# One layer with two token mixers on one core: the second half's output projection as seven block products, with weight sums, a scaled x and another chunk order

## The chip, the core and the metric

The kernel runs on one core of one Trainium2 chip. The metric is the device time of one execution in microseconds, the median of a few runs. TensorE (PE) multiplies, VectorE (DVE) and ScalarE (ACT) do elementwise work and empty PSUM, GpSimd (POOL) does elementwise work on SBUF, and SyncE (SP) issues nearly all DMAs, in order, each after the semaphores that it waits for.

## What is computed

The reference, cut to its skeleton (2048 tokens, width 2048, float32):

```
h = rms_norm(x, norm_w)
q, k, v, z_attn, u, z_ssm = split(h @ w_in)
o_attn = sliding_window_attention(q, k, v) * silu(z_attn)        # 16 heads, 4 kv heads, blocks of 128
y = gelu(ssm(u));  y = y * sigmoid(y @ w_glu + b_glu)            # 64 groups, complex diagonal state
o_ssm = y * silu(z_ssm)
merged = concat(rms_norm(o_attn, g_a), rms_norm(o_ssm, g_s))     # 1024 + 1024 columns
out = x + merged @ w_out                                         # w_out 2048 x 2048
```

## The kernel before

Tokens are worked on in two halves of 1024. Every float32 operand of a large product is cut into a high part (a cast to the fast matmul type, on ACT) and a low part (the rest, a subtraction on DVE); a product is three matmuls: high by high, high by low, low by high. Weights arrive as pieces of 256 KB in a tile `wr` (three buffers) in `w_unit` (lines 310 to 319), and become `wh` and `wl`. With `panel_feat` a piece feeds 24 matmuls of 512 columns, with `panel_tok` 48 of 256 columns.

`run` (lines 1013 to 1070) lays down panels and side work, which `weave` spreads over them with a raised priority; a list scheduler then fixes the order on each engine. In order of time:

- First half: the input projection, beside `setup_all` (line 1078): the rotary tables, the statistics of the second half's x (`x_stats`) and `ssm_setup` (line 580), whose last part (lines 743 to 768) builds the tables `TCS` in DRAM.
- Attention of the first half beside the panels of z. Between the two halves `x_later` (line 297) makes the second half's x: a row of 1/rms spread over the partitions by eight small matmuls (`spread`), then for each of 16 tiles a load of `xT`, a scaling on DVE, a cast on ACT and a subtraction on DVE.
- The second half's projections beside `ssm_pairs`, which leaves y in the order of chunks: a column is (t, c), and token 8c + t.
- For each half: `glu` (line 903) with `tail_attn` (line 872) as side work, both emptying into tiles that `split` cuts in two. In `glu` the tile `tt` has one buffer and is written twice for each half panel; y stays in chunk order until `split`, which reorders.
- The first half's output projection (`out_panel`), beside the second half's attention; the second half's (`out_wide`, line 957), which has PE to itself: 4 column blocks x 2 halves of K x 8 k x 8 row blocks x 3 = 1536 matmuls of 512 columns. The norms' row scales are applied to the finished sums, as they are read from PSUM, by one DVE instruction with x as the addend (line 977).

All loads and stores stand in one queue, SP's, in the scheduler's order.

## Time and profile before

| | |
|---|---|
| median of 3 runs | 2885.39 us (2884.41 to 2886.68) |
| profiled execution | 2888.56 us, span 2886.8 us |
| PE busy | 2801.0 us, 97% of the span |
| DVE, ACT, POOL busy | 1897.9, 961.3, 205.0 us |
| granted TensorE clock, mean | 0.992 |
| HBM traffic | 271.03 MB read, 99.55 MB written |

A view by windows gives the busy time of each engine in a stretch, with the number of instructions, the granted clock as a share of 2.4 GHz, the share of the DMA engines' time and their rate. In a timeline each line is a start, a duration, the engine, the line of the program and what is written and read; in square brackets stands the idle time before it and what ended it. SPq is SP's queue: its duration is that of issuing, not of the transfer.

### The profile page before, as it was taken

To read this page: it belongs to the slowest core of one execution; us is meant where nothing else is said; L and a number is where in the kernel's file an instruction comes from. 1 tells how busy PE (TensorE), PEld (TensorE's weight loads), DVE (VectorE), ACT (ScalarE), POOL (GpSimd) and SP (SyncE) were. 2 spreads that over 40 slices of the span, in tenths; PEclk is the share of its full clock that TensorE was granted. 3 is DMA by queue.
4 is the path that set the end of the run, shared out by engine and by line. 5 is a ranking of instruction groups with operands and counts; after the bars stand their busy time and mean duration, and the time that the engine had idled before them with its cause. 6 is when DMAs were issued, how large, how long until landed. Compare 5 with 4: busy or idle time off the path is not lost.

```text
span 2886.8 us, 45269 instructions
## 1 busy us (share of the span) xinstructions
PE 2801.0 (97%) x16992; PEld 2502.2 (87%) x16992; DVE 1897.9 (66%) x4419; ACT 961.3 (33%) x2089; POOL 205.0 (7%) x341
## 2 busy tenths in 40 slices
PE   6989999989999899999999999998999999999999
PEld 5879999878888688888999988878999999778887
DVE  6682746856773976677679985378999884842222
ACT  6421212134442543333323332345444433521110
POOL 0000000001110112000000000000222220000000
PEclk9999999999999999999999999999999999999999
DMA  5842536553332532544355555343444436333321
GB/s 175 237 117 69 158 92 168 142 142 112 94 115 75 183 115 84 159 144 146 120 156 148 154 156 145 101 138 96 136 143 124 124 106 186 107 104 106 106 78 57
DMA packets 421290, 369.34 MB, mean 128 GB/s; under 512 B 53200, under 2 KB 377296, under 8 KB 421072
## 3 DMA queue, kind: packets, MB, share of 16 engines
q1 hardware_dynamic: 419008, 366.45, 42.9%
q8 instruction: 134, 2.20, 0.3%
q14 instruction: 84, 0.69, 0.1%
q10 hardware_dynamic: 2064, 0.01, 0.0%
HBM read 271.03 MB, written 99.55 MB: 128 GB/s over the span
## 4 chain that ended last, share of the span: by engine, by line
PE 81%; DVE 9%; DMA 6%; issue 2%; ACT 1%; SPq 1%; ACTq 0%; DVEq 0%; POOL 0%; POOLq 0%
PE psg L331 31%; PE psg L349 30%; PE psg L966 6%; PE pss L966 3%; DMA oa<-OA 2%; PE pso L562 2%; PE pss L522 2%; PE pst L966 2%; PE pso L966 1%; DVE ml L93 1%; DVE yg L84 1%; PE pst L547 1%; PE pss L797 1%; DVE wl L84 1%; DVE accs L84 1%
## 5 line engine op out<-in xcount | busy, mean ns | idle before, releaser
L84 DVE TENSOR_TENSOR wl<-wr,wh 128x512 fp32r<-128x512 f32 x456 | 314.6, 690 | 539.6 <-ACT wh L317 530.4
L317 ACT CAST wh<-wr 128x512 fp32r<-128x512 f32 x456 | 282.6, 620 | 1028.3 <-PE psg L331 331.6
L331 PE MATMUL psg<-xl,wh 128*128 128x512 f32 x1536 | 495.3, 395 | 5.2 <-DVE xl L84 5.2
L331 PE MATMUL psg<-xh,wl 128*128 128x512 f32 x1536 | 493.1, 394 | 4.8 <-DVE wl L84 4.7
L331 PE MATMUL psg<-xh,wh 128*128 128x512 f32 x1536 | 492.1, 395 | 3.0 <-ACT wh L317 2.4
L349 PE MATMUL psg<-wh,xh 128*128 128x256 f32 x1536 | 434.2, 284 | 1.8 <-ACT rx L395 1.8
L349 PE MATMUL psg<-wl,xh 128*128 128x256 f32 x1536 | 435.1, 284 | 0.3 <-DVE wl L84 0.3
L349 PE MATMUL psg<-wh,xl 128*128 128x256 f32 x1536 | 433.5, 284 | 0.0
L331 PEld LDWEIGHTS psg<-xl,wh 128*128 128x128 f32 x1536 | 287.9, 189 | 63.7 <-DVE xl L84 7.2
L331 PEld LDWEIGHTS psg<-xh,wl 128*128 128x128 f32 x1536 | 287.5, 189 | 63.0 <-DVE wl L84 6.6
L331 PEld LDWEIGHTS psg<-xh,wh 128*128 128x128 f32 x1536 | 288.0, 190 | 60.8 <-ACT wh L317 3.3
L349 PE MATMUL psg<-wh,mh 128*128 128x256 f32 x1024 | 289.5, 286 | 8.6 <-ACT tt L914 7.7
L349 PEld LDWEIGHTS psg<-wh,xh 128*128 128x128 f32 x1536 | 293.8, 192 | 2.1 <-ACT rx L395 2.0
L349 PEld LDWEIGHTS psg<-wl,xh 128*128 128x128 f32 x1536 | 294.3, 192 | 0.7 <-DVE wl L84 0.7
L349 PEld LDWEIGHTS psg<-wh,xl 128*128 128x128 f32 x1536 | 293.5, 192 | 0.0
L349 PE MATMUL psg<-wl,mh 128*128 128x256 f32 x1024 | 289.7, 284 | 0.7 <-DVE wl L84 0.7
L349 PE MATMUL psg<-wh,ml 128*128 128x256 f32 x1024 | 288.4, 285 | 0.0
L84 POOL TENSOR_TENSOR pm<-ph,sel 128x256 fp32r<-128x256 f32 x240 | 193.1, 825 | 957.6 <-ACT ph L550 612.9
L349 PEld LDWEIGHTS psg<-wh,mh 128*128 128x128 f32 x1024 | 194.7, 191 | 9.4 <-ACT tt L914 7.9
L349 PEld LDWEIGHTS psg<-wl,mh 128*128 128x128 f32 x1024 | 195.9, 191 | 0.9 <-DVE wl L84 0.9
L349 PEld LDWEIGHTS psg<-wh,ml 128*128 128x128 f32 x1024 | 194.7, 191 | 0.0
L539 ACT ACTIVATE sm<-pss,mx,rs 128x128 f32<-128x128 f32 x240 | 108.3, 458 | 93.6 <-DVE mx L93 87.7
(396 smaller groups left out, 4606.6 us busy)
## 6 DMA issues: line engine op xcount, KB each, us to landing
wr<-in_w_in_dram SPq DMA_DIRECT2D x296, 256.0 KB
wr<-in_w_out_dram SPq DMA_DIRECT2D x128, 256.0 KB
tb<-TCS SPq DMA_DIRECT2D x64, 256.0 KB
xr<-in_x_dram SPq DMA_DIRECT2D x64, 256.0 KB
out_dram<-xr SPq DMA_DIRECT2D x64, 256.0 KB
raw<-MBC SPq DMA_DIRECT2D x32, 384.0 KB
kst<-KK SPq DMA_DIRECT2D x56, 192.0 KB
xst<-in_x_dram SPq DMA_DIRECT2D x16, 512.0 KB
```

The costliest lines, as they stand in the source:

```text
L84: (eng or self.nc.vector).tensor_tensor(out=out, in0=a, in1=b, op=op)
L93: self.nc.vector.scalar_tensor_tensor(out=out, in0=a, scalar=s, in1=b, op0=op0, op1=op1)
L317: nc.scalar.copy(hi, raw)
L331: nc.tensor.matmul(ps[t], wt[:, kk, :], xx[k][:, t * 512:(t + 1) * 512], start=(k == 0 and i == 0), stop=(k == nkc - 1 and i == 2))
L349: nc.tensor.matmul(o, xx[k][:, sl], wt[:, kk, :], start=(k == 0 and i == 0 and t % 2 == 0), stop=(k == nkc - 1 and i == 2), skip_group_che ...
L522: nc.tensor.matmul(ps[:, h * 256:h * 256 + 256], qst[:, bq % 2, hp * 2 + h, :], kst[:, i, ksl], start=(h == 0 and i == 0), stop=(i == 1), ...
L539: nc.scalar.activation(sm[:, h, :], sc[:, h, :], AF.Exp, scale=rs[:, h:h + 1], bias=negm[:, h:h + 1], accum_out=den[:, h:h + 1])
L547: nc.tensor.transpose(pt[:, h * P:(h + 1) * P], sm[:, h, :], self.ident)
L562: nc.tensor.matmul(po, vst[:, blk + kb, :], pm[:, i, kb], start=(i == 0 and kb == 0), stop=(i == 1 and kb == 1))
L797: nc.tensor.matmul(o, m[:, g, 0:128], u[:, g, 384:640], start=(g == 0 and i == 0), stop=(i == 2), skip_group_check=True)
L966: nc.tensor.matmul(ps[t], xx[k0 + k][:, t * P:(t + 1) * P], wt[:, 0, :], start=(k == 0 and j == 0), stop=(k == 7 and j == 2))
```

## The change

The second half's output projection is cut into 2 x 2 blocks of tokens, K and columns (each 512 x 1024 x 1024) and computed by the scheme of Strassen and Winograd: seven products in place of eight, with sums of weight blocks and of activation blocks as operands. `product` works one off in two column blocks of 512: 16 weight pieces of 256 KB, 12 matmuls of 512 columns for each; 7 x 16 x 12 = 1344 matmuls in all.

- The four sums of weight blocks (`out_sums`) are made beside `ssm_setup`, three steps for each of its steps, in 32 units (8 K-tiles x 4 pieces of 256 columns): 6 loads, 4 subtractions on POOL and 4 stores of 128 KB a unit, through two tiles `ws0` and `ws1` of one buffer each, into `WT` in DRAM.
- The scales of the norms can no longer be applied to finished sums. So `attn_scale` multiplies the attention output by its row scale on POOL during the first half's last panel and stores it (`OAN`); the sum of squares for it is gathered in `attend` (`asq`). The SSM part is scaled in `ssm_side`. The `form_...` generators make the left operands as side work of the products.
- Finished blocks are kept in `ac` tiles; `final` adds the last product to them on DVE, and x on POOL.
- `x_scaled` makes x times 1/rms for the second half beside the tables (POOL, to `XN` in DRAM); `x_later` then loads it and needs one ACT and one DVE instruction for a tile.
- `glu` writes its result into the tile of z, in token order, so that `split` no longer reorders; `tt` is written once for each half panel.
- `attend`: the mask on the probabilities is applied to one of the two key blocks, with the difference of the values (`dv`) as the other operand: two masked products in place of four, one on POOL and one on DVE; the division by the denominator moves from DVE to ACT. The second half's attention is spread over the first 0.7 of the panels, from 0.5.

```diff
-    def x_later(self, half, pool):
+    def x_scaled(self, pool, half):
         rb = pool.tile([P, HT], F32, tag="rb", name="rb")
         self.spread(self.rstd[:, half * 8:half * 8 + 8], rb, pool)
         for k in range(NK):
+            x = pool.tile([P, HT], F32, tag="xs", name="xs", bufs=2)
+            self.ld.dma_start(x, self.a["xT"][k * P:(k + 1) * P, half * HT:half * HT + HT])
+            self.tt(x, x, rb, ALU.mult, self.nc.gpsimd)
+            self.st.dma_start(self.XN[k], x)
+            yield
+
+    def x_later(self):
+        nc = self.nc
+        for k in range(NK):
             x = self.stage("xq")
-            self.ld.dma_start(x, self.a["xT"][k * P:(k + 1) * P, half * HT:half * HT + HT])
-            self.stt(x, x, self.nw[:, k:k + 1], rb, ALU.mult, ALU.mult)
-            nc.scalar.copy(self.xh[k], x)
-            self.tt(self.xl[k], x, self.xh[k].bitcast(F32), ALU.subtract)
+            self.ld.dma_start(x, self.XN[k])
+            w = self.nw[:, k:k + 1]
+            nc.scalar.activation(self.xh[k], x, AF.Copy, scale=w)
+            self.stt(self.xl[k], x, w, self.xh[k].bitcast(F32), ALU.mult, ALU.subtract)
...
+    def attn_scale(self, pool):
+        for k in range(8):
+            o = self.stage("on")
+            self.ld.dma_start(o, self.OA[k * P:(k + 1) * P, HT:SEQ])
+            self.tt(o, o, self.rba, ALU.mult, self.nc.gpsimd)
+            self.st.dma_start(self.OAN[k], o)
+            yield
...
+    def form_s2(self):
+        for k in range(8):
+            o = self.attn_scaled(k, 0, HT)
+            a1, a2 = o[:, 0:512], o[:, 512:HT]
+            w, wn = self.aow[:, k:k + 1], self.aown[:, k:k + 1]
+            self.stt(a2, a2, w, self.ssm_view(k, 1), ALU.mult, ALU.add)
+            self.stt(a1, a1, wn, a2, ALU.mult, ALU.add)
+            self.split_to(0, k, a1)
+            v = self.ssm_view(k, 0)
+            self.tt(v, v, a1, ALU.subtract)
+            yield
...
+    def out_sums(self, pool):
+        nc = self.nc
+        g = nc.gpsimd
+        for u in range(32):
+            k, c = u // 4, u % 4 * 256
+            x, y = (pool.tile([P, 256], F32, tag=f"ws{i}", name=f"ws{i}") for i in range(2))
+            get = lambda t, q: self.ld.dma_start(t, self.w_block(q, k, c, 256))
+            put = lambda i, t: self.st.dma_start(self.WT[i, k, :, c:c + 256], t)
+            get(x, 1)
+            get(y, 0)
+            self.tt(x, x, y, ALU.subtract, g)
+            put(0, x)
+            get(y, 3)
+            self.tt(y, y, x, ALU.subtract, g)
+            put(1, y)
+            yield
+            get(x, 2)
+            self.tt(x, y, x, ALU.subtract, g)
+            put(3, x)
+            get(x, 1)
+            get(y, 3)
+            self.tt(y, y, x, ALU.subtract, g)
+            put(2, y)
+            yield
...
+    def product(self, slot, q, evac, *sides):
+        for n in range(2):
+            ps = [self.psg() if n == 0 else self.psa() for t in range(4)]
+            for k in range(8):
+                raw = self.wp.tile([P, 512], F32, tag="wr", name="wr")
+                self.ld.dma_start(raw, self.w_block(q, k, n * 512, 512))
...
+                for t in range(4):
+                    sl = slice(o + t * P, o + t * P + P)
+                    for j, (xx, wt) in enumerate(((self.sh[c], hi), (self.sh[c], lo), (self.sl[c], hi))):
+                        nc.tensor.matmul(ps[t], xx[:, sl], wt, start=(k == 0 and j == 0), stop=(k == 7 and j == 2))
...
+            for t in range(4):
+                evac(n, t, ps[t])
...
+        B11, B12, B21, B22, T1, T2, T3, T4 = range(8)
+        ssm, s2, s1 = ssm_side(), self.form_s2(), self.form_s1()
+        s4, a22 = self.form_view(2, 0), self.form_view(0, 1)
+        self.product(0, B11, e1, (self.form_s3(), 8, 0), (ssm, 5, 6))
+        self.product(1, T3, e7, (ssm, 5, 0), (s2, 3, 10))
+        self.product(2, B21, e2, (s2, 5, 0))
+        self.product(0, T2, e6, (s1, 8, 0))
+        self.product(1, T1, e5, (s4, 8, 0))
+        self.product(2, B22, e3, (a22, 8, 0))
+        self.product(0, T4, e4)
...
                 zv = sz.rearrange("p (c t) -> p t c", t=8)[:, t * 4:t * 4 + 4, :]
-                ov = o.rearrange("p (t c) -> p t c", t=4)
-                self.tt(ov, ov, zv, ALU.mult)
-                f = lambda x: x.rearrange("p (c t) -> p t c", t=8)[:, t * 4:t * 4 + 4, :]
+                self.tt(zv, o.rearrange("p (t c) -> p t c", t=4), zv, ALU.mult)
+                if t == 0:
+                    return
                 if m == 0:
-                    nc.scalar.activation(f(acc), ov, AF.Square)
+                    nc.scalar.activation(acc, sz, AF.Square)
                 else:
-                    nc.scalar.activation(tt, o, AF.Square)
-                    self.tt(f(acc), f(acc), tt.rearrange("p (t c) -> p t c", t=4), ALU.add)
+                    sq = self.stage("sq")
+                    nc.scalar.activation(sq, sz, AF.Square)
+                    self.tt(acc, acc, sq, ALU.add)
...
+        with self.tc.tile_pool(name="bg", bufs=1) as pool:
+            sums = self.out_sums(pool)
+            for _ in self.ssm_setup():
+                for _ in range(3):
+                    next(sums, None)
+                yield
```

What the scheduler makes of it is shown at two places. The first is SP beside the SSM setup: `MBC<-Bm` and `MBC<-Cm` are stores of `ssm_setup`, `wr<-in_w_in_dram` are the weight pieces that PE lives on. Before:

```order
L314 DMA wr_3499<-in_w_in_dram 128x2x256 [waits DMAHW7_49,DVE_49]
L724 DMA MBC_85<-Bm_3282 128x4x128 [waits DMAHW0_49,Activation_49]
L731 DMA MBC_85<-Cm_3734 128x4x128 [waits DMAHW1_49,DVE_49]
L314 DMA wr_3553<-in_w_in_dram 128x2x256 [waits DMAHW2_49,DVE_49]
L724 DMA MBC_85<-Bm_3489 128x4x128 [waits DMAHW3_49,Activation_49]
L731 DMA MBC_85<-Cm_3985 128x4x128 [waits DMAHW4_49,DVE_49]
L468 DMA VS_84<-vs_3292 128x2x512 [waits DMAHW5_49,DVE_49]
L468 DMA VS_84<-vs_3296 128x2x512 [waits DMAHW6_49,DVE_49]
L724 DMA MBC_85<-Bm_3730 128x4x128 [waits DMAHW7_49,Activation_49]
```

and in the changed kernel, one unit of `out_sums` from its first load to its last store:

```order
L1005 DMA ws0_3776<-in_w_out_dram 128x256 [waits DMAHW5_49]
L1005 DMA ws1_3777<-in_w_out_dram 128x256 [waits DMAHW2_49,DMAHW0_49]
L1006 DMA WT_90<-ws0_3776 128x256 [waits DMAHW3_49,Pool_49]
L1005 DMA ws1_3777<-in_w_out_dram 128x256 [waits DMAHW4_49,DMAHW2_49]
L323 DMA wr_4872<-in_w_in_dram 128x2x256 [waits DVE_49]
L1006 DMA WT_90<-ws1_3777 128x256 [waits DMAHW6_49,Pool_49]
L1005 DMA ws0_3776<-in_w_out_dram 128x256 [waits DMAHW7_49,DMAHW3_49]
L323 DMA wr_4926<-in_w_in_dram 128x2x256 [waits DVE_49]
L1006 DMA WT_90<-ws0_3776 128x256 [waits DMAHW1_49,Pool_49]
L1005 DMA ws1_3777<-in_w_out_dram 128x256 [waits DMAHW6_49]
L1005 DMA ws0_3776<-in_w_out_dram 128x256 [waits DMAHW1_49]
L1006 DMA WT_90<-ws1_3777 128x256 [waits DMAHW4_49,Pool_49]
```

A store to `WT` waits for POOL (`Pool`), and so for the loads ahead of it; the load into `ws1` in the second row waits for the store ahead of the unit to have landed (`DMAHW0`), and the load into `ws0` in the last but one for the store two rows ahead of it (`DMAHW1`). Two weight pieces stand behind these waits in the same queue.

The second place is ACT at the end of the second half's `glu`, up to the first casts of the output projection's weights (`tt` lines 914 and 924 before; 1160 after). Before:

```order
L869 ACTIVATE mh14_27091<-yg6_25864,sow_613 128x4x128
L924 ACTIVATE tt_26929<-yg6_25864 128x512
L869 ACTIVATE mh14_27091<-yg6_25864,sow_613 128x4x128
L317 CAST wh_27202<-wr_27200 128x512
L914 ACTIVATE tt_27009<-psg_26947,bgh_617 128x512
L924 ACTIVATE tt_27009<-yg7_25870 128x512
L869 ACTIVATE mh15_27097<-yg7_25870,sow_613 128x4x128
L914 ACTIVATE tt_27015<-psg_26948,bgh_617 128x512
L924 ACTIVATE tt_27015<-yg7_25870 128x512
L869 ACTIVATE mh15_27097<-yg7_25870,sow_613 128x4x128
L317 CAST wh_27232<-wr_27230 128x512
L317 CAST wh_27262<-wr_27260 128x512
```

and now:

```order
L1160 ACTIVATE tt_27673<-psg_27611,bgh_619 128x512
L1160 ACTIVATE tt_27677<-psg_27612,bgh_619 128x512
L1171 ACTIVATE sq_27681<-sz_27609 128x1024
L1043 CAST wh_27793<-wr_27791 128x512
L929 ACTIVATE fh3_27686<-ob_27684,aow_613 128x512
L1043 CAST wh_27818<-wr_27816 128x512
L1160 ACTIVATE tt_27754<-psg_27692,bgh_619 128x512
L1160 ACTIVATE tt_27758<-psg_27693,bgh_619 128x512
L1171 ACTIVATE sq_27762<-sz_27690 128x1024
L929 ACTIVATE fh3_27686<-ob_27765,aow_613 128x512
L1043 CAST wh_27836<-wr_27834 128x512
L1043 CAST wh_27859<-wr_27857 128x512
```

The two tanh of a panel (`tt<-psg`, which free its two banks) now follow one another, with no `split` of y between them, and the weights of the first product are cast ahead of the last panel's tanh.

## Rows read from the trace of the kernel before

**Rows 1.** The profile's page: its first line and two lines of section 1.

```profile
span 2886.8 us, 45269 instructions
PE 2801.0 (97%) x16992; PEld 2502.2 (87%) x16992; DVE 1897.9 (66%) x4419; ACT 961.3 (33%) x2089; POOL 205.0 (7%) x341
```

**Rows 2.** Windows of 72 us: stretch, length, PE, PEld, DVE, ACT, POOL busy (instructions), clock, DMA.

```profile
936.00:1008.00 72.00, 60.67 (x278) 47.87 (x277) 64.21 (x121) 35.89 (x74) 11.61 (x10) 0.95 0.61 187
1008.00:1080.00 72.00, 72.00 (x359) 60.78 (x359) 51.33 (x158) 32.48 (x99) 11.83 (x16) 0.98 0.38 109
```

**Rows 3.** The same view, the ends of the two `glu` stages.

```profile
1872.00:1944.00 72.00, 68.63 (x300) 55.87 (x299) 50.39 (x60) 36.85 (x54) 0.00 (x0) 1.00 0.46 145
1944.00:2016.00 72.00, 62.14 (x437) 58.32 (x436) 58.63 (x111) 37.51 (x62) 0.20 (x1) 0.95 0.33 97
2448.00:2520.00 72.00, 68.07 (x303) 55.28 (x302) 57.24 (x66) 39.88 (x58) 0.00 (x0) 1.00 0.38 117
2520.00:2592.00 72.00, 65.31 (x278) 52.57 (x278) 38.62 (x67) 21.66 (x29) 0.00 (x0) 0.93 0.31 101
```

**Rows 4.** The same view with 20 us windows, short idle times at full clock.

```profile
580.00:600.00 20.00, 16.46 (x72) 12.98 (x70) 10.78 (x13) 1.25 (x2) 0.00 (x0) 1.00 0.60 159
```

**Rows 5.** Waits of PE: who waited for whom, us in total, times, longest.

```profile
PE psg L331 <- ACT tt L914: 8.6, 7, 1.7
PE psg L349 <- ACT tt L914: 7.7, 1, 7.7
```

**Rows 6.** Timeline of PE in `out_wide`, the first and last of 29 lines.

```profile
2699.63 0.39 PE L966 MATMUL psg<-wl,mh 128*128 128x512 f32 x1
...
2705.97 0.39 PE L966 MATMUL pss<-wh,ml 128*128 128x512 f32 x1
```

**Rows 7.** The page, section 5: subtraction and cast of a weight piece.

```profile
L84 DVE TENSOR_TENSOR wl<-wr,wh 128x512 fp32r<-128x512 f32 x456 | 314.6, 690 | 539.6 <-ACT wh L317 530.4
L317 ACT CAST wh<-wr 128x512 fp32r<-128x512 f32 x456 | 282.6, 620 | 1028.3 <-PE psg L331 331.6
```

**Rows 8.** Timelines of SP and DVE: two stores and the instructions that wait for them.

```profile
345.15 0.36 SPq L731 DMA_DIRECT2D MBC<-Cm  x1
348.32 0.69 DVE L84 TENSOR_TENSOR Cm<-C,PR 128x512 f32<-128x512 f32 x1 [1.14 <-DMA MBC<-Cm]
367.62 0.37 SPq L731 DMA_DIRECT2D MBC<-Cm  x1
369.92 0.69 DVE L84 TENSOR_TENSOR Cm<-C,PR 128x512 f32<-128x512 f32 x1 [1.01 <-DMA MBC<-Cm]
```

**Rows 9.** Timelines of SP and ACT: two loads and the instructions that wait for them.

```profile
597.17 0.39 SPq L314 DMA_DIRECT2D wr<-in_w_in_dram  x1
600.84 0.62 ACT L317 CAST wh<-wr 128x512 fp32r<-128x512 f32 x1 [9.64 <-DMA wr<-in_w_in_dram]
2452.34 0.32 SPq L879 DMA_DIRECT2D oa<-OA  x1
2456.29 1.34 ACT L869 ACTIVATE mh<-oa,aow 128x512 fp32r<-128x512 f32 x2 [0.88 <-DMA oa<-OA]
```

**Rows 10.** DMA issues: sizes; then the weight pieces in the window 220 to 620 us.

```profile
MBC<-Cm SPq DMA_DIRECT2D x16, 256.0 KB
oa<-OA SPq DMA_DIRECT2D x16, 512.0 KB
wr<-in_w_in_dram SPq DMA_DIRECT2D x63, 256.0 KB
```

**Rows 11.** Windows of 72 us, the stretch with the highest DMA rate.

```profile
72.00:144.00 72.00, 71.67 (x324) 58.94 (x324) 49.06 (x150) 30.68 (x56) 1.55 (x36) 1.00 0.86 236
```

**Rows 12.** Instructions on the tile `pm`: POOL's durations in ns, min/median/max.

```profile
L84 POOL TENSOR_TENSOR pm<-ph,sel x240: 724/742/2300, 639.9 to 2365.9; 128x256 fp32r<-128x256 f32 x120
```

**Rows 13.** The chain of waits, its last piece.

```profile
2877.76 5.51 DVE xr L93 x8
```

**Rows 14.** Instructions of line 281, the matmuls of `spread` into one bank.

```profile
L281 PE MATMUL pss<-diag,ones x8: 271/275/377, 944.5 to 947.2; 128*128 128x128 f32 x8
```

More of the change, by code (lines that the diff above doesn't have):

```diff
@@ L575, in attend @@
                 t0 = (b - 1) * P
+                if half:
+                    sq = pool.tile([P, 2, 256], F32, tag="sq", name="sq")
+                    nc.scalar.activation(sq, oT, AF.Square)
+                    acc = self.asq[:, t0 - HT:t0 - HT + 256]
+                    if g == 0:
+                        self.tt(acc, sq[:, 0], sq[:, 1], ALU.add, nc.gpsimd)
+                    else:
+                        for c in range(2):
+                            self.tt(acc, acc, sq[:, c], ALU.add, nc.gpsimd)
                 self.st.dma_start(self.OA[g * 256:g * 256 + 256, t0:t0 + 256].rearrange("(c p) t -> p c t", p=P), oT)
@@ L767, in ssm_setup @@
                             tb[gg * 64:gg * 64 + 64])
+                for _ in range(4):
+                    next(xs, None)
                 yield
@@ L854, in row_scale, with split @@
         return r
-    def split(self, k, src, w, perm):
-        nc = self.nc
+    def split(self, k, src, w):
         self.xh[k] = self.xt.tile([P, HT], F32R, tag=f"xh{k}", name=f"mh{k}")
@@ new lines, in strassen_out, with part, rows, final @@
+    def strassen_out(self, pool):
+        nc = self.nc
+        acc = {}
+        def part(n, c, t):
+            i = (8 * c + 4 * n + t) // 2
+            if i not in acc:
+                acc[i] = self.xt.tile([P, HT], F32, tag=f"x{'hl'[i // 4]}{12 + i % 4}", name=f"ac{i}")
+            return acc[i][:, (t % 2) * 512:(t % 2) * 512 + 512]
+        e = lambda n, t: part(n, 0, t)
+        v = lambda n, t: part(n, 1, t)
+        def rows(y, r, c, n, t):
+            r0 = HT + r * 512 + t * P
+            return y[0, r0:r0 + 2 * P, c * 1024 + n * 512:c * 1024 + n * 512 + 512].rearrange("(t p) c -> p t c", p=P)
+        xs = {}
+        def final(r, c, n, t, ps, base, keep, op=ALU.add):
+            if t % 2 == 0:
+                x = self.stage("xr").rearrange("p (t c) -> p t c", t=2)
+                xs[0] = x, (self.stage("xo").rearrange("p (t c) -> p t c", t=2) if keep else x)
+            x, o = xs[0]
+            v = o[:, t % 2] if keep else base
+            self.tt(v, base, ps, op)
+            if t % 2 == 0:
+                self.ld.dma_start(x, rows(self.a["x"], r, c, n, t))
+            self.tt(x[:, t % 2], x[:, t % 2], v, ALU.add, nc.gpsimd)
+            if t % 2:
+                self.st.dma_start(rows(self.out, r, c, n, t - 1), x)
+        def e1(n, t, ps):
+            nc.scalar.copy(e(n, t), ps)
+        def e7(n, t, ps):
+            self.tt(v(n, t), e(n, t), ps, ALU.add)
+        def e2(n, t, ps):
+            final(0, 0, n, t, ps, e(n, t), True)
+        def e6(n, t, ps):
+            self.tt(e(n, t), e(n, t), ps, ALU.add)
+            self.tt(v(n, t), v(n, t), ps, ALU.add)
+        def e5(n, t, ps):
+            self.tt(e(n, t), e(n, t), ps, ALU.add)
+            final(1, 1, n, t, ps, v(n, t), True)
+        def e3(n, t, ps):
+            final(0, 1, n, t, ps, e(n, t), False)
+        def e4(n, t, ps):
+            final(1, 0, n, t, ps, v(n, t), False, ALU.subtract)
+        def ssm_side():
+            self.rss = self.row_scale(pool, self.gacc, 0.125, "rs")
+            yield
+            self.rbs = pool.tile([P, HT], F32, tag="rba", name="rbs")
+            self.spread(self.rss, self.rbs, pool)
+            yield
+            yield from self.form_ssm()
+        B11, B12, B21, B22, T1, T2, T3, T4 = range(8)
[8 more added lines that the diff above has]
+        self.product(0, T4, e4)
@@ L931, in glu @@
             pass
+        if half:
+            self.yg, self.gacc = out, acc
+            return
         for m in range(8):
-            self.split(k0 + m, yg[m], self.sow[:, m:m + 1], True)
+            self.split(k0 + m, out[m], self.sow[:, m:m + 1])
         self.rss = self.row_scale(pool, acc, 0.125, "rs")
```

168 lines of the change are left out of this document (108 added, 60 removed).

## The prediction

> **What bounds the kernel now.** I read the page first [rows 1]: PE is busy for 2801.0 of 2886.8 us, DVE for two thirds, so the end is PE's, and a change pays by matmuls that it removes, by idle time of PE that it closes, and by idle time that it opens. The windows show where the idle time is: in the input projection's change of halves, 936 to 1008 us, PE lacks 11.3 us and DVE is at 64.2 of 72 [rows 2]; at the ends of the two `glu` stages it lacks 3.4 + 9.9 and 3.9 + 6.7 us [rows 3]. There the granted clock is also below 1, which costs its missing share of the stretch: 0.05 and 0.02 of 72 us in rows 2 (5.0 us), 0.05 and 0.07 in rows 3 (8.6 us). PE's waits name a cause for `glu`: 16.3 us on the tanh of line 914 [rows 5]. Short idle times alone leave the clock up: 3.5 us of 20 at 1.00 [rows 4]. Everywhere else PE is fed, through one queue: all weight pieces come through SP, and 400 us of the input projection used 63 of them [rows 10], one in 6.35 us.
>
> **The change, part by part.** The sum starts from the profiled execution, 2888.6 us, which lies 3.2 above the median.
>
> *Seven products.* 1344 matmuls of 512 columns take the place of 1536. In `out_wide` 28 starts lie in 2705.97 - 2699.63 = 6.34 us, 0.2264 us each [rows 6]; 192 fewer are **-43.5 us**, all on the path, since PE has that stage to itself.
>
> *Feeding them.* A weight piece now lasts for 12 matmuls, 2.72 us, half as long as before. Cast and subtraction of a piece take 0.62 and 0.69 us [rows 7], the load some 3.7 us in traffic [rows 9]: 5.0 us, through three buffers 1.7 us a piece, so the supply holds as long as nothing in SP, ACT or DVE keeps a piece waiting for more than 3 us. DVE has 16 x 0.69 = 11 us of weights in a product of 43.5 us, and the `form_` and evacuation work adds up to some 23 us more; the longest runs of it, three or four instructions of 0.7 to 1.2 us, come near those 3 us. I take **+12 us** of slips over 112 pieces (0 to 40).
>
> *The change of halves.* A tile of x costs DVE one instruction in place of two, 16 fewer of the 1024-column kind (twice the 0.69 us of 512 columns [rows 7], less the overhead: about 1.2 us), 19 us, and the eight matmuls of `spread` go from there. With DVE no longer full, of the 16.3 us (11.3 idle, 5.0 of clock) [rows 2] I expect 7 to stay, for the first tiles' loads: **-9 us** (-16 to 0).
>
> *The ends of `glu`.* On ACT two tanh of a panel now stand together, ahead of the squares; before, the second tanh stood behind the square and the splits of y, whose turn came only when DVE let go of `tt`. For the second half no split of y is left, for the first they are of contiguous columns. Of 32.5 us (23.9 idle, 8.6 of clock) [rows 3] I take 20 back and leave 12, the first half's splits among them: **-20 us** (-28 to -5).
>
> *Spreads and the tail.* Two spreads more than before, in `run` and in `ssm_side`; one bank's worth runs from 944.5 to 947.2 us [rows 14], so a spread is 5.4 us, partly beside other matmuls: **+6 us** (2 to 11). At the end, x was added by DVE in the pass that read PSUM, eight instructions in 5.5 us [rows 13]; now four sums on DVE are followed by four of 512 columns on POOL, at twice the 0.74 us of 256 columns [rows 12], 5.9 us, before the last store can go: **+4 us** (2 to 7).
>
> *Attention.* One masked product and the division leave DVE and POOL; PE has the same four matmuls. PE did not wait there, so nothing is counted.
>
> *The weight sums beside the SSM setup.* They have no PE work, and 128 subtractions on POOL, idle there, would be hidden. What counts is their 320 DMAs in SP's queue. The order rows show one unit as a chain, in which the queue stops at each step: a store lands, a load, a subtraction, a load, a subtraction, a load, a subtraction, a store lands, a load, a subtraction, each waiting for the one ahead. That is 4 loads, 2 landings of stores and 4 subtractions, and the weight pieces stand behind those waits: 70 of them in the 27 units outside the tables' part, 2.6 a unit. No row shows a load of 128 KB, so I scale: the highest rate is 236 GB/s at 0.86 of the engines' time [rows 11], 274 GB/s. A load of 512 KB alone took 2456.29 - 2452.34 = 3.95 us [rows 9, 10], 1.91 of it transfer, so 128 KB take 2.04 + 0.48 = 2.5 us. A store of 256 KB took 369.92 - 367.62 = 2.30 us [rows 8, 10], so 128 KB take 1.8. With 0.74 us for a subtraction [rows 12] a unit lasts 10.1 + 3.6 + 3.0 = 16.7 us. PE eats 2.6 pieces in 14.1 us at 24 matmuls of 0.2264 us, or in 16.5 at the 6.35 us that setup work and all took before; I take 15.3. So the queue is slower than PE by 1.4 us a unit, 38 us in 27 units, less about two pieces of 5.4 us in hand: **+27 us**. The low end is 0 (at 14.1 us a unit). For the high end I take the slower rows: a load of 256 KB in traffic 3.67 us [rows 9], so 3.2 for half; a store with another behind it 3.17 [rows 8], so 2.7; with 0.74 a unit is 21.2 us, +5.9 a unit, +150. Below nothing is excluded: nothing leaves this queue there. I stay near the low rows, since a unit's transfers go one at a time and are small, and keep the slow ones for the range.
>
> The Trainium skill, "DMA: Bandwidth & Descriptors", section "Latency and other measured facts", gives an access latency of HBM of 0.2 us on average and 2 us at high load; by it each of the six transfers of the chain could grow by up to 1.8 us, an estimate of 10.8 us a unit more, about 290 us over 27 units. The rows above, with 0.9 us between a quiet store and one in traffic [rows 8], show half of that at most; the price of the crowded case is taken from rows alone.
>
> *The scaled x.* 32 DMAs of 512 KB beside the tables, 16.8 MB, are 61 us of transfer at 274 GB/s over four units with 27 weight pieces, 150 us or more; that can delay pieces behind the stores of the tables: **+6 us** (0 to 20).
>
> Sum: 2888.6 - 43.5 + 12 - 9 - 20 + 6 + 4 + 27 + 6 = 2871, on the median 2868. I forecast **2869 us**.
>
> **The rivals.**
> (1) *The chain is covered.* A unit takes no longer than PE's share (14 to 15 us); the sums cost at most 10 us: 2832 to 2853, say 2842. For it: POOL is idle, a quiet store takes 2.3 us. Against it: already the quiet loads give 16.7.
> (2) *The queue is crowded*, and slower than before. SP's waits become the bound of the input projection: a unit of 19 to 21.2 us against 15.3 adds 100 to 159 us, less 11 in hand, to the 2838 that is left without the sums and x: 2930 to 2990, say 2950. It ends above before once a unit is over 17.6 us (27 x 2.3 + 6 - 11 = 57 against the 50 saved). For it: six transfers in series through the same engines that carry pieces, tables and x, and a POOL instruction that took up to 2.3 us [rows 12]; against it the quiet rows.
> (3) *The products starve.* If each piece comes 0.6 us late, 112 cost 67 us in place of 12: 2924. For it: half the cover for each piece; against it, the 1.7 us a piece above.
>
> **How the numbers follow.** The forecast's own case runs from 2853 to 2900 (a unit of 16.2 to 17.9 us) and has 0.38; rival 1 has 0.32, rival 2 0.22, rival 3 0.08. About 0.2% is what a measurement of this kernel can tell from no change: 2879.6 to 2891.2. Faster: all of rival 1, and 0.21 of the forecast's case, 0.53; same 0.09; slower 0.38. The range leaves out the lowest 0.08 of rival 1 and the upper half of rival 2: 2836 to 2952.
>
> **What would show it.** In the windows from 150 to 700 us: PE busy near 72 speaks for rival 1, 66 to 70 for the forecast, under 62 for rival 2, with waits of ACT's cast on `wr` as the sign, and the interval between first loads of neighbouring units (16.7 us) as the measure. In the products: 0.2264 us between matmuls and gaps of PE below 15 us in all; PE's waits on line 914's successor under 5 us; the last sum on POOL 6 us after the last matmul. The prediction is wrong if the stage from 150 to 700 us grows by over 60 us, or if the products take over 330 us.

## The result, and the profile after the change

The changed kernel takes 3050.16 us (median, 3042.32 to 3056.01) beside 2886.03 us for the kernel before: 1.0564 times as long, 95% interval 1.0552 to 1.0576. The forecast was 2869 us, the range 2836 to 2952; the result is 181 us above the one and 98 us above the upper end of the other. The mechanism is that of rival 2 (the queue is crowded), but it makes only a part of the 181 us. The profiled execution took 3042.32 us, its span is 3040.6 us. The page's first line and its line on PE answer to [rows 1]: PE is as busy as before, although it has 192 matmuls of 512 columns fewer to do in the last projection (the mean granted clock is 0.965 in place of 0.992), and 153 us more of the span pass without it (238.8 us in place of 85.8).

```profile
span 3040.6 us, 46262 instructions
...
PE 2801.8 (92%) x16832; PEld 2502.2 (82%) x16832; DVE 1879.5 (62%) x4271; ACT 1082.8 (36%) x2453; POOL 422.8 (14%) x528
```

To see where the time went I compare when the same instruction starts in each trace (us from the span's start; worked out from the traces; the runs in the three columns on the right are told below):

```
                                    before   after    sums    sums on      best
                                                      out     POOL, spread kernel
first store of v (VS)                333.4   388.5    331.5    341.2      340.5
last store of q (QS), first half     570.5   701.2    600.4    613.9      595.1
last z of the first half (ZS)        947.8  1107.6    994.3    999.7      969.5
second u, second half (US)          1021.8  1162.7   1050.3   1053.6     1037.6
last but one z, second half (ZS)    1849.6  2026.8   1871.6   1877.6     1865.1
30th of 32 stores of attention (OA) 2338.3  2507.1   2355.0   2356.0     2345.0
first matmul, last projection       2520.5  2712.0   2557.9   2559.2     2531.7
end of the span                     2886.8  3040.6   2889.1   2892.5     2860.1
```

Read the "after" column against "before": the lag is 55, 131, 160, 141, 177, 169, 191.5 and 153.8 us. So the stage with the weight sums loses 160 us, the change of halves gives back 19, the second half's projections lose another 36, the first `glu` and the panels behind it give back 8, the last panel and the second `glu` lose 23, and the seven products give back 38. Five windows of 72 us in the first stage, and the change of halves, which answers to [rows 2] (columns as there):

```profile
144.00:216.00 72.00, 56.72 (x239) 45.68 (x238) 55.17 (x224) 12.21 (x22) 12.84 (x15) 0.88 0.57 156
288.00:360.00 72.00, 50.24 (x369) 49.46 (x368) 30.84 (x58) 11.45 (x20) 12.20 (x15) 0.86 0.40 122
360.00:432.00 72.00, 58.23 (x469) 57.88 (x468) 40.85 (x61) 13.03 (x29) 11.30 (x13) 0.88 0.66 199
504.00:576.00 72.00, 42.38 (x306) 41.80 (x306) 31.55 (x92) 4.38 (x8) 14.81 (x14) 0.77 0.59 153
864.00:936.00 72.00, 42.87 (x185) 34.55 (x184) 16.55 (x47) 16.47 (x47) 8.74 (x15) 0.76 0.49 139
1080.00:1152.00 72.00, 69.47 (x349) 58.08 (x348) 57.48 (x135) 47.60 (x111) 14.76 (x19) 1.00 0.68 217
```

The kernel before, at the same times in the stage into which the sums went:

```profile
144.00:216.00 72.00, 64.27 (x288) 52.80 (x287) 58.60 (x247) 14.68 (x26) 0.85 (x1) 0.93 0.43 117
288.00:360.00 72.00, 71.36 (x613) 71.18 (x612) 52.21 (x89) 16.96 (x35) 0.00 (x0) 1.00 0.53 160
360.00:432.00 72.00, 72.00 (x606) 72.00 (x605) 33.39 (x70) 14.30 (x26) 0.00 (x0) 1.00 0.31 89
504.00:576.00 72.00, 68.59 (x405) 60.54 (x404) 60.52 (x174) 12.73 (x20) 0.45 (x4) 1.00 0.52 144
576.00:648.00 72.00, 63.19 (x296) 52.42 (x296) 43.17 (x113) 22.41 (x67) 3.17 (x5) 0.95 0.51 142
```

In the changed kernel no engine is full in the first five windows, the DMA engines are at half of their time, and the granted clock (1.00 is the 2.4 GHz level throughout, lower means part of the stretch at 1.2) is down where PE stood idle. ACT's waits and SP's own waits over the whole span (who waited for whom, us in total, times, longest) say what the engines stood for:

```profile
ACT wh L326 <- DMA wr<-in_w_in_dram: 388.4, 63, 16.3
```

```profile
SPq L1006 <- POOL ws L87: 313.9, 116, 5.0
...
SPq L1005 <- DMA WT<-ws: 55.9, 56, 3.8
```

The casts of weights, ahead of every matmul, waited 388 us for their pieces (29.5 us in the kernel before). SP, which issues the pieces, meanwhile stood 314 us at stores of sums (L1006) until POOL had subtracted, and 56 us at loads (L1005) until a store had landed. From 216 to 432 us alone it waited 128 us for the sums and 1.7 us for a buffer of `wr` to come free, and its issues took 73 us; in the kernel before it waited 114 us for free buffers there, and its issues took 30 us. SP's timeline shows one unit of the sums:

```profile
264.77 0.66 SPq L323 DMA_DIRECT2D wr<-in_w_in_dram  x1
266.54 0.33 SPq L1006 DMA_DIRECT2D WT<-ws  x1
266.95 0.45 SPq L1005 DMA_DIRECT2D ws<-in_w_out_dram  x1
270.91 0.33 SPq L1006 DMA_DIRECT2D WT<-ws  x1
271.29 0.42 SPq L1005 DMA_DIRECT2D ws<-in_w_out_dram  x1
271.81 0.39 SPq L323 DMA_DIRECT2D wr<-in_w_in_dram  x1
274.91 0.33 SPq L1006 DMA_DIRECT2D WT<-ws  x1
275.34 1.66 SPq L1005 DMA_DIRECT2D ws<-in_w_out_dram  x2
277.05 0.43 SPq L323 DMA_DIRECT2D wr<-in_w_in_dram  x1
279.88 0.33 SPq L1006 DMA_DIRECT2D WT<-ws  x1
```

Each load is followed about 4 us later by the store of its result, and between the two SP does next to nothing: a piece of w_in goes out only where the order put one, at 264.77, 271.81 and 277.05. ACT's timeline of the same stretch has the other end of it; each cast starts as its piece lands, after 5 to 9 us of idle time:

```profile
268.94 0.62 ACT L326 CAST wh<-wr 128x512 fp32r<-128x512 f32 x1 [9.07 <-DMA wr<-in_w_in_dram]
274.83 0.62 ACT L326 CAST wh<-wr 128x512 fp32r<-128x512 f32 x1 [5.27 <-DMA wr<-in_w_in_dram]
281.96 0.62 ACT L326 CAST wh<-wr 128x512 fp32r<-128x512 f32 x1 [6.51 <-DMA wr<-in_w_in_dram]
```

### The profile page after: what moved, and what is told of

Its sections match the earlier page's. It is cut to its first block, busy times and chain, and to the rows that moved or that the text cites. A ratio compares the mean times of both kernels' runs of the same rounds, so it can differ in the third digit from the quotient of the medians.

```text
span 3040.6 us, 46262 instructions
## 1 busy us (share of the span) xinstructions
PE 2801.8 (92%) x16832; PEld 2502.2 (82%) x16832; DVE 1879.5 (62%) x4271; ACT 1082.8 (36%) x2453; POOL 422.8 (14%) x528
## 5 line engine op out<-in xcount | busy, mean ns | idle before, releaser
L87 DVE TENSOR_TENSOR wl<-wr,wh 128x512 fp32r<-128x512 f32 x504 | 369.7, 736 | 608.9 <-ACT wh L326 469.9
L326 ACT CAST wh<-wr 128x512 fp32r<-128x512 f32 x392 | 242.4, 619 | 879.2 <-DMA wr<-in_w_in_dram 388.4
L340 PE MATMUL psg<-xh,wh 128*128 128x512 f32 x1536 | 498.4, 399 | 25.5 <-ACT wh L326 24.8
L358 PE MATMUL psg<-wl,xh 128*128 128x256 f32 x1536 | 441.5, 288 | 20.4 <-DVE wl L87 20.4
L358 PE MATMUL psg<-wh,xh 128*128 128x256 f32 x1536 | 440.8, 288 | 9.1 <-ACT rx L404 9.1
L358 PE MATMUL psg<-wh,xl 128*128 128x256 f32 x1536 | 439.8, 288 | 0.0
L358 PEld LDWEIGHTS psg<-wl,xh 128*128 128x128 f32 x1536 | 300.7, 196 | 21.2 <-DVE wl L87 21.1
L358 PEld LDWEIGHTS psg<-wh,xh 128*128 128x128 f32 x1536 | 300.4, 196 | 9.4 <-ACT rx L404 9.3
L87 POOL TENSOR_TENSOR ws<-ws,ws 128x256 f32<-128x256 f32 x128 | 118.5, 926 | 537.8 <-DMA ws<-in_w_out_dram 472.0
L87 POOL TENSOR_TENSOR pm<-ph,sel 128x256 fp32r<-128x256 f32 x120 | 92.0, 767 | 442.2 <-ACT ph L571 435.4
```

Source lines behind the costliest of these rows:

```text
L87: (eng or self.nc.vector).tensor_tensor(out=out, in0=a, in1=b, op=op)
L326: nc.scalar.copy(hi, raw)
L340: nc.tensor.matmul(ps[t], wt[:, kk, :], xx[k][:, t * 512:(t + 1) * 512], start=(k == 0 and i == 0), stop=(k == nkc - 1 and i == 2))
L358: nc.tensor.matmul(o, xx[k][:, sl], wt[:, kk, :], start=(k == 0 and i == 0 and t % 2 == 0), stop=(k == nkc - 1 and i == 2), skip_group_che ...
```

## Experiments

**Theories at the start.** A: SP's in-order queue holds the weight pieces while the chain of the sums waits. B: the sums' 42 MB slow the pieces on the DMA engines. C: POOL's subtractions slow DVE's part of the pieces. D: something else in the change (scaled x, later attention).

**Sums out.** Only the sums go; the four products that used them read plain blocks of `w_out` in their place (the output is then no longer the layer's), and everything else of the change stays.

```diff
-        if q > 3:
-            return self.WT[q - 4, k, :, c0:c0 + n]
+        q = q % 4
...
-            sums = self.out_sums(pool)
+            sums = iter(())
```

> The changed kernel without the block that forms the sums of output weights; the four products that used the sums read plain blocks of w_out instead (same number and size of weight pieces), so this part of the result is left out. The store ZA 3 left 138 us later in the changed kernel than before, the first tanh half 177 us later. If the sums, by whatever way, make all of that: 3050 - 177 = 2870, range 2845 to 2885, and the wait of the weight casts on pieces of w_in falls from 388 us to under 60. If scaled x beside the tables or the later attention has a share of its own: 2900 to 2980.

2890.96 us, 1.0012 times before (1.0003 to 1.0021). So the sums cost 3050.2 - 2891.0 = 159 us, 18 less than I expected, and the rest of the change, on which I had counted for 44 us, gains nothing. The casts' wait on pieces of w_in fell to 77 us, not under 60. The two profiles lie 151 us apart: 117 us are idle time of PE, and 34 us are the same matmuls taking longer at a lower clock (PE busy 2767.7 us without sums, mean clock 0.984, against 2801.8 and 0.965). By the starts above, 113 us of the sums' price arise up to the last z of the first half, and 43 more in the second half's projections. The third column also shows where the gain of the rest went: +46.5 us up to the last z of the first half, -18 at the change of halves, -12 from there to the last stores of attention, +21 between these and the products, -35 in the products.

**The old kernel with the sums added**, `out_sums` run beside `ssm_setup` as in the change:

> The kernel before with the block of weight sums alone added beside the SSM setup; the sums go to DRAM and nobody reads them. If the sums alone make the loss up to the first tanh half (177 us, with 16 to 28 of it from the clash of late scans with the K panel): 2886 + 150 to 190 = 3036 to 3076. If they need the rest of the change (scaled x, the spread's DMAs) to hurt: 2930 to 3000.

3089.57 us, 1.0696 times before (1.068 to 1.0712): 201 us for the sums alone, above what I expected. They need nothing else of the change to hurt. They cost 42 us more here than in the changed kernel, and not at the same places: the lag over the kernel before is 183 us at the last z of the first half, 206 at the second u, and then stays (204 at the last but one z), while in the changed kernel the sums' share is 113, 112 and 155 us. Why the first stage loses 70 us more here I have not settled.

**The same sums from POOL's queue.**

```diff
-            get = lambda t, q: self.ld.dma_start(t, self.w_block(q, k, c, 256))
-            put = lambda i, t: self.st.dma_start(self.WT[i, k, :, c:c + 256], t)
+            get = lambda t, q: g.dma_start(t, self.w_block(q, k, c, 256))
+            put = lambda i, t: g.dma_start(self.WT[i, k, :, c:c + 256], t)
```

> The changed kernel with the ten transfers of each unit of sums issued from POOL's queue instead of SP's: same bytes, same subtractions, same chain, but no weight piece stands behind a wait of theirs. Theory A (the in-order SP queue holds the pieces while a store waits for POOL or a load for a store): 2860 to 2900. Theory B (the 42 MB themselves, on the 16 DMA engines, slow the pieces): 3010 to 3060, little changed. Theory C (POOL's subtractions slow the casts' differences on DVE): 3010 to 3060 too.

3117.05 us, 1.0794 times before (1.0773 to 1.0816): slower still, so theory A in this simple form fell. But the windows say more than the total:

```profile
288.00:360.00 72.00, 71.89 (x617) 71.69 (x617) 57.52 (x100) 17.59 (x36) 23.31 (x38) 1.00 0.67 209
360.00:432.00 72.00, 72.00 (x607) 72.00 (x606) 37.52 (x73) 13.68 (x25) 27.04 (x40) 1.00 0.49 145
432.00:504.00 72.00, 42.96 (x361) 42.76 (x359) 18.45 (x46) 9.61 (x16) 21.30 (x34) 0.82 0.63 169
936.00:1008.00 72.00, 34.53 (x153) 28.26 (x151) 7.24 (x11) 6.33 (x11) 25.83 (x44) 0.76 0.29 81
```

From 216 to 432 us PE is full at full clock, with the sums' transfers and subtractions beside it: B and C are out there. Then the wait has only moved. A unit took 28.3 us from POOL's queue (24.3 from SP's; first load to last store, divided by 32), so the sums lasted to 1033 us, and now POOL, in order too, kept others waiting: DVE's waits from 420 to 600 us hold a table's first column, which POOL sets, and PE's from 900 to 1250 us the first half's attention, whose tiles come free only when the sums are done.

```profile
DVE Ct L87 <- POOL St L779: 50.2, 1, 50.2
```

```profile
PE pst L501 <- DMA kst<-KK: 71.7, 1, 71.7
```

SP's longest single wait, 62.5 us, ties the two: the load of that k stood for the last stores of sums.

```profile
SPq L492 <- DMA WT<-ws: 65.7, 2, 62.5
```

**Theory A, second form:** the price is the length of the sums' own chain, a unit's waits times 32, and it is paid by whichever in-order queue carries it, and by whoever waits for its end. Then both must change: the chain must have slack between its steps, and it must not stand in the queue of the weights.

**Spread sums, on SP.** Four tiles a unit in place of two, so that all four blocks are loaded at once (four loads in place of six), subtracted a panel step later and stored one step after that. The sums' steps now go with the panels, no longer with the SSM setup. The new loop:

```diff
+        for u in range(32 + 1):
+            if u:
+                put(u - 1, ws)
+            if u == 32:
+                return
+            ws = get(u)
+            yield
+            sub(ws)
             yield
```

> The changed kernel with the sums left in the stage of the SSM setup but spread over the panel steps, four loads, four subtractions and four stores each a step apart on four tiles instead of two, all still on SP's queue. Theory A (SP stands in the serial chain): PE above 66 of 72 us in the windows from 216 to 504 where the changed kernel has 50 to 64, total 2890 to 2930. If transfers or POOL cost PE directly in this place: windows as in the changed kernel, 2990 to 3050.

2943.65 us, 1.0197 times before (1.0182 to 1.0213). Two thirds of the price are gone, but two of the four windows from 216 to 504 did not reach 66; the scheduler brought the units together, one in 9.0 us (median), so they were over at 424 us:

```profile
288.00:360.00 72.00, 53.61 (x398) 53.01 (x398) 33.28 (x58) 10.82 (x19) 27.77 (x34) 0.86 0.57 174
360.00:432.00 72.00, 55.36 (x442) 54.84 (x441) 43.09 (x60) 13.02 (x29) 21.34 (x24) 0.86 0.76 233
```

**Spread sums, on POOL's queue.** The same, with `self.ld` and `self.st` of these eight transfers turned into `g`:

> The run with the sums spread over the panel steps of the SSM setup (four tiles, four loads, four subtractions and four stores a unit), with all eight transfers of a unit moved from SP's queue to POOL's. On SP the unit took 9 us and PE still had only 53 to 70 of 72 us from 144 to 432, with SP waiting 65 us for POOL and 22 us for stores in 216 to 432. If it is SP's queue that starves PE there: PE 70 to 72 in each of these windows, as the first run on POOL's queue had, and 2890 to 2905 in all, the time without sums. If the transfers do it, whoever issues them: windows of 53 to 62 and 2935 to 2950, as on SP. If POOL, carrying 12 us a unit, is late for the table memsets: PE falls in 432 to 648 instead, 2910 to 2940.

2891.5 us, 1.0017 times before (1.0006 to 1.0028): the time without sums (2890.96). In its own stage it is 5 to 13 us behind that run (table of starts, first three rows), which the rest makes up. The same windows:

```profile
288.00:360.00 72.00, 68.63 (x585) 68.00 (x585) 56.50 (x93) 16.95 (x35) 42.68 (x66) 1.00 0.72 226
360.00:432.00 72.00, 72.00 (x606) 72.00 (x606) 43.77 (x79) 13.55 (x24) 48.11 (x76) 1.00 0.63 193
```

SP's own waits from 216 to 432 us, first of the run on SP, then of this one, show the difference at its place:

```profile
SPq L1021 <- POOL ws L87: 64.5, 69, 2.6
SPq L1008 <- DMA WT<-ws: 22.2, 26, 2.9
SPq L323 <- DVE wl L87: 3.7, 1, 3.7
```

```profile
SPq L323 <- DVE wl L87: 103.1, 29, 6.3
```

`SPq L323 <- DVE wl` is the healthy wait: the next piece is ready to go and stands for a free buffer. Where it is near zero, SP is behind PE. With the two earlier runs this makes a table of two changes, in us (2891 without sums). The right column also has four loads a unit in place of six, and its sums start at 77 to 78 us instead of 125 to 128:

```
              chain as in the change   chain spread, four tiles
on SP                3050.2                   2943.7
on POOL's queue      3117.1                   2891.5
```

The 52 us between the two on the right come from one edit, the queue; with it the scheduler also set the units further apart (11.8 us in place of 9.0, median). The Trainium skill, "DMA: Bandwidth & Descriptors", section "Issuing engines are not separate DMA queues", says that several issuing engines save only the time that a sequencer takes to issue, usually little beside the transfer. The transfers did share their engines here (from 288 to 360 us share 0.72 and 226 GB/s on POOL's queue, more than on SP's). But what SP was spared has two parts. Of these 216 us its issues took 106 us with the sums in its queue and 34 us without them: that is the part which the section names, and it is not little here. Its waits for POOL and for stores took 87 us and then none: weight pieces stood behind instructions that wait, and this part the section does not name. SP had next to no slack left (3.7 us for a free buffer); whether taking away one of the two parts alone would have been enough these runs don't tell.

**Spread sums on SP, beside the first half's attention instead** (seven tiles, over the z and u panels):

> The changed kernel with the weight sums taken out of the SSM setup and put beside the first half's attention (z panels of the SSM gate and the first u panels of the next half), one unit in two panel steps, its four loads, four subtractions and four stores each a step apart, so that SP waits for nothing; four loads a unit instead of six. Theory A, refined after the first runs (what costs is the length of the unit's own chain, 24 us beside SP and 28 us from POOL's queue, times 32, paid by whichever in-order queue carries it): as without sums, 2885 to 2915. If the transfers (34 MB here) or POOL's subtractions cost PE directly: 2930 to 3050.

2925.52 us, 1.0133 times before (1.0118 to 1.0148), between the two bands, 10 above that of theory A. The first sums were brought forward into the stage of the tables; from 440 to 760 us SP stood 50.6 us for POOL's subtractions and the casts 119 us for pieces. Another place doesn't cure it either.

**The last panel's hole.** In the changed kernel PE stood 17.2 us there for DVE's residual sums. DVE's timeline around it:

```profile
2577.38 1.23 DVE L96 SCALAR_TENSOR_TENSOR yl<-yg,yh 128x1024 fp32r<-128x1024 f32 x1 [0.59 <-ACT yh L1142]
2579.16 2.79 DVE L96 SCALAR_TENSOR_TENSOR yl<-yg,yh 128x1024 fp32r<-128x1024 f32 x1 [0.56 <-ACT yh L1142]
2581.87 2.83 DVE L87 TENSOR_TENSOR wl<-wr,wh 128x512 fp32r<-128x512 f32 x1
2584.62 6.63 DVE L96 SCALAR_TENSOR_TENSOR yl<-yg,yh 128x1024 fp32r<-128x1024 f32 x2
...
2598.15 3.23 DVE L96 SCALAR_TENSOR_TENSOR xr<-psg,rar,xr 128x256 f32<-128x256 f32 x8 [6.29 <-issue]
```

DVE is slow up to 2591 (POOL multiplies from 2577.95 to 2590.18, 12.23 us for four tiles `on`), then idle; the sums start when x has come. First the stores of `on` moved to POOL's queue:

```diff
-            self.st.dma_start(self.OAN[k], o)
+            self.nc.gpsimd.dma_start(self.OAN[k], o)
```

> The changed kernel with the eight stores of the scaled attention (OAN) issued from POOL's queue instead of SP's. In its trace PE stands 17.2 us at the last panel of the first half's output projection, waiting for DVE's residual sums, whose x loads are issued at 2592.9 behind stores that wait for POOL. If the queue makes that hole: 3050 - 12 to 18 = 3032 to 3038. If DVE makes it (its differences took 2.8 us there instead of 0.7 and 1.2 while POOL multiplied): 3045 to 3055, unchanged.

3056.44 us, 1.0582 times before (1.0563 to 1.06): no gain, the queue is not the cause here. In that trace, too, the four loads of x for the panel were issued only from 2606.1 to 2610.9, one by one as the stores of `on` (2600.5 to 2604.9) let go of their tiles: `on` and `xr` share the four staging buffers. With the tiles of `on` taken from the GLU's pool (tested beside other edits, told below):

```diff
-            o = self.stage("on")
+            o = pool.tile([P, HT], F32, tag=("zn0", "zn1", "accs")[k % 3], name="on")
```

> The one before with the eight tiles of the scaled attention taken from three tiles of the GLU's pool instead of the four staging buffers. Moving their stores to POOL's queue left the 17 us hole as it was, and in that trace the four x loads of the last panel are issued only as those four buffers come free. If the buffers make the hole: minus 12 to 19, near 2853. If DVE beside POOL makes it: minus 0 to 4.

2937.52 us, 1.0173 times before (1.0158 to 1.0188): 11.2 us less than the same kernel without this edit (2948.67, next paragraph), a little under the band; in the second pair, `e12_all` below, 17.0 us. The wait on the residual sums, 16 to 18 us in all runs of the changed kernel without this edit, is 3.0 there and in `e12_all`. So the buffers make most of the hole.

**The scaled x.** It was undone (x scaled at the change of halves, on DVE, as before), first on top of the sums beside the attention:

> The one before with the scaled x beside the tables undone: x of the second half is scaled where the old kernel did it, on DVE (its row of factors in a staging buffer). Without sums the store QS 4 to 7 and OA 0 fell 37 us behind the old kernel in the stage of tables, and the change of halves gave back 16 to 20. If scaled x makes these 37: the kernel before this one minus 15 to 25, near 2870. If the tables' stage lost them for another reason: plus 10 to 20, near 2910.

2948.67 us, 1.0208 times before (1.019 to 1.0225): 23 us slower, against both readings. It was no clean question: the sums then took more of the stage of tables (from 440 to 760 us SP stood 75.4 us for POOL's subtractions instead of 50.6), and they had six tiles instead of seven. On top of the spread sums on POOL's queue it was one:

> The one before with the scaled x beside the tables undone (x of the second half scaled at the change of halves, on DVE, as in the old kernel). Clean repeat of the question that the earlier one could not answer because the sums then fell into the same stage: if scaled x makes the 37 us lost in the stage of tables without sums, this is 15 to 25 us faster than the one before (37 saved, 16 to 20 given back); if the tables' stage loses them anyway, 10 to 20 us slower.

2882.58 us, 0.9986 times before (0.9975 to 0.9997): 8.9 us faster, less than the 15 to 25 that I expected. The starts have its two parts: the last z of the first half comes 32 us earlier (967.6 instead of 999.7), and 14 of these go back at the change of halves, where the second u starts at 1035.7 instead of 1053.6. Of the 46.5 us that the run without sums lost up to the last z, 32 are thus the scaled x; the other 14 stay open. SP's waits in the run without sums, from 440 to 760 us, name the same cause as for the sums, stores and loads that wait:

```profile
SPq L306 <- POOL xs L87: 46.5, 11, 14.0
SPq L304 <- DMA XN<-xs: 19.4, 7, 5.2
```

**All three edits.**

> The one before with the eight tiles of the scaled attention taken from the GLU's pool instead of the staging buffers, which gave 11 us in the earlier pair. Expected: 10 to 18 us faster than the one before; with all three edits 2850 to 2875, faster than the kernel before the change by 0.4 to 1.2%.

2865.61 us, 0.9929 times before (0.9911 to 0.9947): the best kernel of the study, 0.7% faster than before and 184.6 us faster than the change. **Scaled x put back, on POOL's queue:**

> The best run so far (sums on POOL's queue, scaled attention in the GLU's tiles) with the scaled x put back beside the tables, its 32 transfers too on POOL's queue instead of SP's. Without sums SP waited 66 us in that stage for POOL's products of x and for their stores. If these waits of SP made the 37 us there, and not POOL beside DVE: 2866 minus 10 to 18, 2848 to 2856, since the change of halves stays short. If POOL, in order too, now keeps the tables' first columns waiting, or slows DVE: 2866 to 2880, no gain.

2875.08 us, 0.9954 times before (0.9941 to 0.9968): 9.5 us slower than without it. SP's waits for it from 440 to 760 us are 10.7 us instead of 66, but the stage of tables is not whole either: the last z comes 18 us later than in the best kernel, and 9 of these come back at the change of halves. Whether that is POOL's order or its sharing with DVE (last section) these runs don't tell.

## Why the prediction was wrong, point by point

**The weight sums** are the step that failed: a unit of 16.7 us, and so +27 us (0 to 150). The unit took 20.3 us and the sums cost 159 us, 113 in their own stage and most of the rest later, for which the sum had no term. The order of the unit's chain was read rightly; its length was not. The page's DMA issues after the change (KB each, median us to landing, of the 20 loads and 20 stores whose landing the trace tells) give a load 2.8 us where I had 2.5, a store 2.0 where I had 1.8:

```profile
ws<-in_w_out_dram SPq DMA_DIRECT2D x192, 128.0 KB, 2.8
WT<-ws SPq DMA_DIRECT2D x128, 128.0 KB, 2.0
```

With subtractions of 0.93 us on average (median 0.74) a unit is 4 x 2.8 + 2 x 2.0 + 4 x 0.93 = 18.9 us, and it took 20.3 as a median (first load to first load) and 24.3 on average, four units in the tables' stage 43 to 52 each. The pieces, stores and loads in between each take SP some 0.4 us of issue and wait for things of their own. I had measured the chain as if SP had nothing else to do. Rows 8 and 9 held the slow values (2.7 and 3.2), and I kept them for the range. The latency at high load of the Trainium skill ("DMA: Bandwidth & Descriptors", section "Latency and other measured facts"), which I cited, would have added up to 1.8 us to each transfer; the trace shows 0.3 and 0.2 more than my estimates, so it was not that which made the unit long.

A reading was wrong as well: "everywhere else PE is fed". In the stage into which I put the sums and the scaled x, PE had idle time and a lowered clock already before the change (64.27 of 72 us at 0.93 from 144 to 216, 63.19 at 0.95 from 576 to 648, above); its supply had no slack to give there.

**Rival 2** had the mechanism and the unit's size (19 to 21.2 us), but its 2930 to 2990 fell 60 us short. Its upper end has 148 us for the sums, which cost 159; 47 of the 60 us lie in what it shares with the forecast, the rest of the change at 2838 (of the profiled execution, 2835 on the median) and 6 for the scaled x, where 2891 was measured. At the measured unit its own sum gives 27 x 5.0 - 11 = 124 us, close to the 113 of the stage, though I had counted idle time alone and the clock is in the 113 (0.76 to 0.88 in the five windows above). What had no term at all is what follows. The sums ended at 904 us and only then let go of memory that the attention needs: its first load goes out at 906 us, as it does 2 us after the last store of sums in the other two runs with the long chain (871 and 1035 us). The first transposes start at 911 us instead of 605, so the first loads of the scan (`ssm_pairs`) came at 1414 us instead of 1173, and the scan met the k panel of the second half. DVE serves both, and PE lost time and clock in two windows of 20 us where it had lost none before:

```profile
1620.00:1640.00 20.00, 12.55 (x86) 11.25 (x84) 18.40 (x32) 7.48 (x14) 0.10 (x1) 0.81 0.48 144
1640.00:1660.00 20.00, 15.37 (x111) 15.37 (x112) 16.95 (x32) 5.95 (x11) 0.10 (x1) 0.76 0.68 231
```

Without the sums the lag falls by 6 us over the second half's projections instead of growing by 36; the clash is theirs. The lead of the scan's first load over the first store of that k panel fits it, though no run tests it alone: 200 us here; 266 (before), 271 (old kernel with the sums) and 307 (sums out), where this stage lost nothing; 161 in the run with the chain on POOL's queue, where it lost 162 us.

**The rest of the change**, -44 us, failed too: it gained nothing. **The scaled x**, +6 us (0 to 20): wrong, about 32 in its stage. **The change of halves**, -9 (-16 to 0): better than I said, -18. Together -3 was said, and undoing both gained 8.9.

**The ends of `glu`**, -20 us (-28 to -5): the cause was right, the gain was not. PE's wait on the tanh is 1.1 us where it was 16.3 [rows 5]:

```profile
PE psg L358 <- ACT tt L1160: 1.1, 1, 1.1
```

The first `glu` gave 5 to 10 us. At the second I missed what the added scaling of the attention does on the panel ahead of it: it takes the staging buffers that the residual x needs, and the stage lost some 20 us instead of gaining 10; the sum had no term for that. Even with other tiles it is 4 us longer than before (2345.0 to 2531.7, against 2338.3 to 2520.5).

**The products**, -43.5 with +12 of slips and +4 at the tail: right, and better than said. From the first matmul to the end of the span 366.4 us became 328.6, -37.8 in place of -27.5 (some 2 us of slips, worked out from these numbers), and 328.4 to 333.4 in the other runs that have them, at the 330 that I had set as the limit. PE waits 9.3 us for pieces in them, most of it here:

```profile
PE pss L1049 <- DVE wl L87: 8.4, 3, 4.2
```

The span ends 7.9 us after the last matmul instead of 4.3, the +4 at the tail. Rival 3 is out. The forecast's own signs spoke as they were set: PE's mean over the windows from 144 to 648 us is 58.7 of 72, under the 62 of rival 2, and the stage grew by 131 us, over the 60.

## What to carry to other kernels

Work that costs the bound engine nothing can still cost its feeder: before a chain of load, compute and store is put into the queue that feeds the matmuls, lay its waits end to end, with the queue's other issues in between, and hold that against the time in which the matmuls use up the pieces that stand between them (here 20 to 24 us against some 15). If it must run, give each step time before the next one needs it, and let a queue carry it that nobody waits for; one of the two alone was not enough (2944 and 3117 us; both together 2891). And in a trace look at what the feeding queue waits for: as long as most of its waiting is for buffers to come free, it is ahead of the matmuls (114 of 216 us before the change); where that wait is near zero (1.7 and 3.7 us here), they starve.

## What the runs showed of the hardware

DVE and POOL hold each other up when both work on SBUF without a break. Above, DVE's `yl` took 2.79 us instead of 1.23 and `wl` 2.83 instead of 0.69 while POOL multiplied. The other way round, in the last run a product of x on POOL, 2.41 us as a median, took 13.08 us; the timeline of POOL, then the first and the last of DVE's instructions beside it:

```profile
540.58 13.08 POOL L87 TENSOR_TENSOR xs<-xs,rb 128x1024 f32<-128x1024 f32 x1 [0.20 <-DMA xs<-in_xT_dram]
```

```profile
540.29 0.68 DVE L87 TENSOR_TENSOR St<-St,uc 128x512 f32<-128x512 f32 x1
...
550.12 1.28 DVE L87 TENSOR_TENSOR wl<-wr,wh 128x512 fp32r<-128x512 f32 x2
```

DVE ran without a gap there and POOL came through only as that ended. The Trainium skill, "Trainium Architecture — The Big Picture", section "What this means for kernel authors", has the two share a port by an exclusive lock, not by a split of bandwidth; the trace agrees for POOL's 13.08 us. On the other hand 34 MB more of transfers, in windows at up to 226 GB/s, cost PE next to nothing once no piece stood behind them (2891.5 us with them, 2891.0 without).
